# Grouped instance norm: 24 of 32 four-megabyte units joined to twelve of 8 MB, loaded as column halves, stored as whole rows

## The chip, the core and the metric

One core of a Trainium2 chip runs the kernel. The time is the device time of one execution, in microseconds; the three runs of the kernel before took 626.78, 626.83 and 626.91 us, median 626.83. The profile is of one further execution, recorded by the hardware profiler.

The engines named here: DVE (VectorE) and ACT (ScalarE) compute on data in SBUF, the on-chip memory of 128 partitions; PE (TensorE) multiplies matrices; POOL (GpSimd) does small set-up work; SP (SyncE) issues transfers. Transfers between HBM, the large memory, and SBUF are issued by SP, ACT or POOL, each on its own queue, and carried out by 16 DMA engines that serve all the queues.

## What is computed

```python
def reference(x, gamma):                       # x: 4 x 8 x 16 x 256 x 256, gamma: 8 x 16, float32
    mu = x.mean(axis=(3, 4), keepdims=True)
    var = ((x - mu) ** 2).mean(axis=(3, 4), keepdims=True)
    x_norm = (x - mu) / np.sqrt(var + 1e-5)
    out = x_norm * gamma[None, :, :, None, None]
    return out.astype(np.float32)
```

Each of the 4 x 8 x 16 = 512 channels has 65536 values (256 KB), is reduced to its mean and variance, and is written back normalised and scaled. Every value is read once and written once: 134.2 MB each way.

## The kernel before

**Tiling.** The input is seen as one flat array, cut into U = 32 units of 4 MB. A unit is 128 rows of F = 8192 values (32 KB); S = 8 rows are one channel, so a unit holds K = 16 channels, and it lies in one piece in HBM. Six SBUF tiles, `slots` (L45), are used in turn: unit u lives in slot u % 6.

**Order.** The order is written out by hand (`manual_schedule`): each engine takes its instructions as the program lists them, and waits where data or a buffer isn't there yet. At the start six loads are issued, those of units 1 and 3 on ACT's queue, the others on SP's (L56-57). Before them POOL issues two small transfers: `touch`, a write of 8 KB to the output (L54), and the load of gamma (L55). Then POOL builds `navg`, a 128 x 128 matrix that is -1/HW within each block of 8 rows (L63-72), and DVE and PE spread gamma over the partitions into `g_col` (L80-91).

**The loop over units** (L104-141), for each unit:

- L106: DVE sums each row. L107: ACT squares it and sums the squares (its full-size output, `junk`, is never read).
- L115: PE multiplies the two columns of sums by `navg`, which gives every row minus its channel's mean and minus its mean square, in PSUM.
- L116: DVE makes minus the variance; L120: ACT takes the root; L124 and L126: DVE inverts it and multiplies by gamma.
- L135: DVE adds minus the mean and multiplies by the scale, in place. In unit 0 alone, 3/8 of the columns go to ACT (L131-134).
- L139: ACT issues the store of the unit on its queue.
- L141: SP issues the load of unit u + 6 into the same slot, which must wait for that store to have landed.

So SP's queue carries the loads (but for two of the first), and ACT's queue all the stores. ACT issues a store only when DVE has finished L135, so the next unit's L107 stands behind it in ACT's program order. On DVE, the next unit's L106 stands behind L135.

Of the kernel before, what the change touches and what calls it, by code (L numbers as in the profile page):

```python
# [1 line left out]

# [4 lines left out]

F32 = mybir.dt.float32
U8 = mybir.dt.uint8
ALU = mybir.AluOpType  # L10
ACTF = mybir.ActivationFunctionType
AX = mybir.AxisListType


@with_exitstack
def kernel(
    ctx: ExitStack,
    tc: tile.TileContext,
    x: bass.AP,
    gamma: bass.AP,  # L20
    out: bass.AP,
):
    nc = tc.nc
    B, G, C, H, W = x.shape
    P = nc.NUM_PARTITIONS
    HW = H * W
    n_ch = B * G * C
    S = 8
    K = P // S
    F = HW // S  # L30
    U = n_ch // K
    NG = (G * C) // K
    AHEAD = 6
    assert HW % S == 0 and (G * C) % K == 0

    xv = x.rearrange("b g c h w -> (b g c h w)").rearrange("(u p f) -> u p f", p=P, f=F)
    ov = out.rearrange("b g c h w -> (b g c h w)").rearrange("(u p f) -> u p f", p=P, f=F)
    gv = gamma.rearrange("g c -> (g c)")

    data = ctx.enter_context(tc.tile_pool(name="data", bufs=1))  # L40
    singles = ctx.enter_context(tc.tile_pool(name="singles", bufs=1))
    psum = ctx.enter_context(tc.tile_pool(name="psum", bufs=4, space=bass.MemoryType.PSUM))
    ctx.enter_context(tc.manual_schedule())

    slots = [data.tile([P, F], F32, name=f"xt{i}") for i in range(AHEAD)]  # L45

    def load(u, queue):
        queue.dma_start(out=slots[u % AHEAD][:], in_=xv[u])  # L48


    g_row = singles.tile([1, G * C], F32, name="g_row")
    touch = singles.tile([16, 128], F32, name="touch")
    nc.vector.memset(touch[:], 0.0)  # L53
    nc.gpsimd.dma_start(out=ov[0][0::S, 0:128], in_=touch[:])  # L54
    nc.gpsimd.dma_start(out=g_row[:], in_=gv[None, :])  # L55
    for u in range(AHEAD):  # L56
        load(u, nc.scalar if u in (1, 3) else nc.sync)

    eps_t = singles.tile([P, 1], F32, name="eps_t")
    nc.gpsimd.memset(eps_t[:], 1e-5)  # L60
    one = singles.tile([1, 1], F32, name="one")
    nc.gpsimd.memset(one[:], 1.0)
    navg = singles.tile([P, K, S], F32, name="navg")  # L63
    nc.gpsimd.memset(navg[:], -1.0 / HW)  # L64
    nc.gpsimd.affine_select(  # L65
        out=navg[:], in_=navg[:], pattern=[[-S, K], [0, S]], compare_op=ALU.is_ge,
        fill=0.0, base=0, channel_multiplier=1,
    )
    nc.gpsimd.affine_select(  # L69
        out=navg[:], in_=navg[:], pattern=[[S, K], [0, S]], compare_op=ALU.is_ge,  # L70
        fill=0.0, base=S - 1, channel_multiplier=-1,
    )
    navg_w = navg[:].rearrange("p k s -> p (k s)")
    root_eps = singles.tile([P, 1], F32, name="root_eps")
    nc.scalar.activation(out=root_eps[:], in_=eps_t[:], func=ACTF.Sqrt)  # L75
    g_rep = singles.tile([1, NG, K, S], F32, name="g_rep")
    g_ps = psum.tile([P, NG], F32, name="g_ps", bufs=1)
    g_col = singles.tile([P, NG], F32, name="g_col")

    nc.vector.tensor_copy(  # L80
        out=g_rep[:],
        in_=g_row[:].rearrange("o (n k) -> o n k", n=NG).unsqueeze(3).to_broadcast([1, NG, K, S]),
    )
    for n in range(NG):
        nc.tensor.matmul(  # L85
            out=g_ps[:, n : n + 1],
            lhsT=g_rep[:, n].rearrange("o k s -> o (k s)"),
            rhs=one[:],
            start=True, stop=True,
        )  # L90
    nc.vector.tensor_copy(out=g_col[:], in_=g_ps[:])  # L91

    junk = singles.tile([P, F], U8, name="junk")

    st = singles.tile([P, U, 2], F32, name="st")
    nvar = singles.tile([P, U], F32, name="nvar")
    std = singles.tile([P, U], F32, name="std")
    rstd = singles.tile([P, U], F32, name="rstd")
    scale = singles.tile([P, U], F32, name="scale")

    shift = singles.tile([P, 1], F32, name="shift")

    squares = []
    for u in range(U):  # L104
        t = slots[u % AHEAD]
        nc.vector.reduce_sum(out=st[:, u, 0:1], in_=t[:], axis=AX.X)  # L106
        square = nc.scalar.activation(  # L107
            out=junk[:], in_=t[:], func=ACTF.Square, accum_out=st[:, u, 1:2],
        )
        if u:  # L110

            tc.declare_no_dep(square.ins, squares[-1].ins, reason="junk, ordered by the root between")
        squares.append(square)
        ps = psum.tile([P, 2], F32, name="ps")
        nc.tensor.matmul(out=ps[:], lhsT=navg_w, rhs=st[:, u], start=True, stop=True)  # L115
        nc.vector.tensor_scalar(  # L116
            out=nvar[:, u : u + 1], in0=ps[:, 0:1], scalar1=ps[:, 0:1],
            scalar2=ps[:, 1:2], op0=ALU.mult, op1=ALU.add,
        )
        nc.scalar.activation(  # L120
            out=std[:, u : u + 1], in_=nvar[:, u : u + 1], func=ACTF.Sqrt,
            bias=eps_t[:], scale=-1.0,
        )
        nc.vector.reciprocal(out=rstd[:, u : u + 1], in_=std[:, u : u + 1])  # L124
        g = u % NG
        nc.vector.tensor_mul(  # L126
            out=scale[:, u : u + 1], in0=rstd[:, u : u + 1], in1=g_col[:, g : g + 1],
        )
        cut = F * 5 // 8 if u == 0 else F
        if cut < F:  # L130
            nc.vector.tensor_mul(out=shift[:], in0=ps[:, 0:1], in1=scale[:, u : u + 1])  # L131
            nc.scalar.activation(  # L132
                out=t[:, cut:], in_=t[:, cut:], func=ACTF.Identity, bias=shift[:], scale=scale[:, u : u + 1],
            )
        nc.vector.tensor_scalar(  # L135
            out=t[:, :cut], in0=t[:, :cut], scalar1=ps[:, 0:1], scalar2=scale[:, u : u + 1],
            op0=ALU.add, op1=ALU.mult,
        )
        nc.scalar.dma_start(out=ov[u], in_=t[:])  # L139
        if u + AHEAD < U:  # L140
            load(u + AHEAD, nc.sync)  # L141


# [1 line left out]
_INS = ['x', 'gamma']  # L145
_OUTS = [((4, 8, 16, 256, 256), 'float32')]


# [23 lines left out]
```

## Time and profile before

| | |
|---|---|
| median of three runs | 626.83 us |
| the profiled execution, first to last instruction | 625.2 us |
| HBM read, written | 134.22 MB, 134.23 MB, 429 GB/s over the span |
| DVE busy | 441.8 us (71%) |
| ACT busy | 241.8 us (39%) |
| PE, POOL busy | 21.4 us, 2.4 us |
| L106, row sums (DVE) | 32 of 8.68 us |
| L107, squares (ACT) | 32 of 7.03 us |
| L135, normalise (DVE) | 31 of 4.55 us, one shorter |
| wait of L106 for loads | 102.2 us in 24 waits |
| wait of L107 for loads | 233.8 us in 24 waits |

The page of a profile shows the span in 40 equal slices (here 15.63 us each), with the mean busy share of the 16 DMA engines in tenths (9 is 90% or more) and what they moved in GB/s. It counts the packets of each DMA queue: q1 is SP's, q10 is ACT's. Its chain of waits goes back from the last instruction to what released it, step by step; lines of the chain read "start, duration, what". "To landing" is the time from the issue of a transfer to the completion signal, so it includes the time that the transfer stands in its queue. In a timeline a line reads "start, duration, engine, line, operation, output<-input", and the bracket is the idle time of that engine just before and what ended it.

### The profile page before, as it was taken

The page shows a single profiled execution, that of the slowest core. Times are in us where ns is not written, and L with a number is a line of the kernel's source. Part 1 is how long each engine was busy: PE and PEld are TensorE (multiplying, and loading weights), DVE is VectorE, ACT ScalarE, POOL GpSimd, SP SyncE. Part 2 cuts the span into 40 slices and gives each one's busy share as a digit, 9 for nine tenths or more (in the row PEclk, how much of TensorE's full clock was granted, in tenths as well). Part 3 has the DMA queues.
Part 4 walks back from the last instruction along what each step waited for, and adds up shares of the span by engine and source line. Part 5 has one row for each costly group of instructions (what it writes and reads, how often), then busy time and mean ns, then how long its engine had stood idle before and what let it go on. Part 6 is the DMA issues. An engine that isn't in the chain of part 4 may idle for free.

```text
span 625.2 us, 635 instructions
## 1 busy us (share of the span) xinstructions
PE 21.4 (3%) x80; PEld 19.5 (3%) x80; DVE 441.8 (71%) x164; ACT 241.8 (39%) x99; POOL 2.4 (0%) x11
## 2 busy tenths in 40 slices
PE   0200000000000000000000000000000000000000
PEld 0200000000000000000000000000000000000000
DVE  0589999998776687666786767867668676687730
ACT  0464444444443244432344423444224442244400
POOL 1000000000000000000000000000000000000000
DMA  8999999999999999999999999999999999999998
GB/s 370 436 407 432 436 436 436 436 436 430 423 436 434 434 428 434 434 436 436 436 436 428 426 436 436 432 430 434 434 436 436 436 436 421 432 436 434 434 430 367
DMA packets 9282, 268.46 MB, mean 429 GB/s; under 512 B 1072, under 2 KB 1088, under 8 KB 1088
## 3 DMA queue, kind: packets, MB, share of 16 engines
q10 hardware_dynamic: 4896, 142.61, 52.9%
q1 hardware_dynamic: 4320, 125.83, 46.8%
q0 software_dynamic: 64, 0.01, 0.0%
q14 instruction: 2, 0.02, 0.0%
HBM read 134.22 MB, written 134.23 MB: 429 GB/s over the span
## 4 chain that ended last, share of the span: by engine, by line
another core or an unknown queue 61%; DMA 17%; DVE 15%; SPq 1%; PE 1%; issue 0%; ACT 0%
DMA xt<-in_x_dram 10%; DVE st L106 10%; DMA out_dram<-xt 8%; DVE xt L135 5%; SPq L48 1%; PE ps L115 1%; ACT std L120 0%; DVE nvar L116 0%; DVE rstd L124 0%; DVE scale L126 0%; DVE shift L131 0%
## 5 line engine op out<-in xcount | busy, mean ns | idle before, releaser
L106 DVE TENSOR_REDUCE st<-xt 128x1 f32<-128x8192 f32 x32 | 277.9, 8684 | 102.2 <-DMA xt<-in_x_dram 102.2
L107 ACT ACTIVATE junk<-xt 128x8192 uint8<-128x8192 f32 x32 | 225.0, 7030 | 272.0 <-DMA xt<-in_x_dram 233.8
L135 DVE TENSOR_SCALAR xt<-xt,ps,scale 128x8192 f32<-128x8192 f32 (+1 forms) x32 | 144.0, 4500 | 1.1
L120 ACT ACTIVATE std<-nvar,eps_t 128x1 f32<-128x1 f32 x32 | 9.4, 295 | 79.4 <-DVE nvar L116 79.4
L115 PE MATMUL ps<-st,navg 128*128 128x2 f32 x64 | 17.8, 348 | 557.3 <-DVE st L106 557.3
L115 PEld LDWEIGHTS ps<-st,navg 128*128 128x128 f32 x64 | 16.0, 310 | 559.1 <-issue 546.2
L116 DVE TENSOR_SCALAR nvar<-ps 128x1 f32<-128x1 f32 x32 | 9.2, 286 | 23.8 <-PE ps L115 23.8
L124 DVE RECIPROCAL rstd<-std 128x1 f32<-128x1 f32 x32 | 5.2, 163 | 11.6 <-ACT std L120 11.6
L80 DVE COPY g_rep<-g_row 1x1024 f32<-1x1024 f32 x1 | 0.7, 681 | 14.4 <-DMA g_row<-in_gamma_dram 14.4
L107 ACT ACTIVATION_READ_ACCUMULATOR junk<-xt 128x1 f32 x32 | 6.0, 186 | 0.0
L126 DVE TENSOR_TENSOR scale<-rstd,g_col 128x1 f32<-128x1 f32 x32 | 5.1, 158 | 1.1
L85 PE MATMUL g_ps<-one,g_rep 1*128 1x1 f32 x16 | 3.5, 347 | 16.3 <-DVE g_rep L80 16.3
L85 PEld LDWEIGHTS g_ps<-one,g_rep 1*128 1x128 f32 x16 | 3.5, 326 | 16.3 <-issue 16.3
L132 ACT ACTIVATE xt<-xt,shift,scale 128x3072 f32<-128x3072 f32 x1 | 2.9, 2947 | 0.7 <-DVE shift L131 0.7
L91 DVE COPY g_col<-g_ps 128x8 f32<-128x8 f32 x1 | 0.2, 167 | 3.7 <-PE g_ps L85 3.7
L75 ACT ACT_TABLE_LOAD x1 | 1.3, 1283 | 1.7 <-PEq L156 1.7
L53 DVE MEMSET touch<- 16x128 f32 x1 | 0.2, 165 | 0.9 <-PEq L156 0.9
L54 POOL DMA_DIRECT2D out_dram<-touch x1 | 0.6, 617 | 0.8 <-DVE touch L53 0.8
L55 POOL DMA_DIRECT2D g_row<-in_gamma_dram x1 | 0.5, 487 | 0.0
L65 POOL TENSOR_SCALAR_AFFINE_SELECT navg<-navg 128x128 f32<-128x128 f32 x1 | 0.4, 400 | 0.1
L69 POOL TENSOR_SCALAR_AFFINE_SELECT navg<-navg 128x128 f32<-128x128 f32 x1 | 0.4, 399 | 0.1
L64 POOL MEMSET navg<- 128x128 f32 x1 | 0.2, 230 | 0.0
(8 smaller groups left out, 1.0 us busy)
## 6 DMA issues: line engine op xcount, KB each, us to landing
out_dram<-xt ACTq DMA_DIRECT2D x32, 4096.0 KB, 62.5
xt<-in_x_dram SPq DMA_DIRECT2D x30, 4096.0 KB, 38.5
xt<-in_x_dram ACTq DMA_DIRECT2D x2, 4096.0 KB, 31.7
out_dram<-touch POOLq DMA_DIRECT2D x1, 8.0 KB, 9.3
g_row<-in_gamma_dram POOLq DMA_DIRECT2D x1, 0.5 KB, 13.5
```

The source lines that it names most:

```text
L48: queue.dma_start(out=slots[u % AHEAD][:], in_=xv[u])
L75: nc.scalar.activation(out=root_eps[:], in_=eps_t[:], func=ACTF.Sqrt)
L85: nc.tensor.matmul(out=g_ps[:, n : n + 1], lhsT=g_rep[:, n].rearrange("o k s -> o (k s)"), rhs=one[:], start=True, stop=True,)
L106: nc.vector.reduce_sum(out=st[:, u, 0:1], in_=t[:], axis=AX.X)
L107: square = nc.scalar.activation(out=junk[:], in_=t[:], func=ACTF.Square, accum_out=st[:, u, 1:2],)
L115: nc.tensor.matmul(out=ps[:], lhsT=navg_w, rhs=st[:, u], start=True, stop=True)
L116: nc.vector.tensor_scalar(out=nvar[:, u : u + 1], in0=ps[:, 0:1], scalar1=ps[:, 0:1], scalar2=ps[:, 1:2], op0=ALU.mult, op1=ALU.add,)
L120: nc.scalar.activation(out=std[:, u : u + 1], in_=nvar[:, u : u + 1], func=ACTF.Sqrt, bias=eps_t[:], scale=-1.0,)
L124: nc.vector.reciprocal(out=rstd[:, u : u + 1], in_=std[:, u : u + 1])
L126: nc.vector.tensor_mul(out=scale[:, u : u + 1], in0=rstd[:, u : u + 1], in1=g_col[:, g : g + 1],)
L132: nc.scalar.activation(out=t[:, cut:], in_=t[:, cut:], func=ACTF.Identity, bias=shift[:], scale=scale[:, u : u + 1],)
L135: nc.vector.tensor_scalar(out=t[:, :cut], in0=t[:, :cut], scalar1=ps[:, 0:1], scalar2=scale[:, u : u + 1], op0=ALU.add, op1=ALU.mult,)
```

## The change

The unit list becomes uneven: four units of 4 MB ("singles"), twelve of 8 MB ("doubles"), and four singles again, 20 in all. F stays 8192. A double is 128 rows of 16384 values (64 KB), four rows to a channel, 32 channels.

- The six slots become three tiles of twice the width (`pairs`). `home(u)` gives a unit's tile and first column: a single takes one half of a tile, a double the whole.
- A double is loaded by two transfers of 4 MB, one for the left and one for the right half of the columns: each reads 32 KB out of every 64 KB of HBM. Each half is reduced and squared when it has come (inner loop over `halves`). PE adds both halves' sums up in one PSUM tile by two matmuls.
- The small steps (variance, root, reciprocal, scale) run once for a double. L135's successor normalises all 16384 columns in one instruction, and one transfer of 8 MB stores them in rows of 64 KB.
- The first loads are those of units 0 to 4: units 0 to 3 are singles and unit 4 is a double, which makes the same six transfers of 4 MB, on the same queues as before.
- A load is issued after the unit whose store frees the last of the halves that it needs. Loads of later doubles come two at a time on SP's queue; where singles follow doubles, the loads of two singles come together.
- The set-up builds `navg` and `g_col` twice, for 8 and for 4 rows to a channel.

```diff
@@ set-up, loads
-    S = 8
-    K = P // S
-    F = HW // S
-    U = n_ch // K
-    NG = (G * C) // K
-    AHEAD = 6
-    assert HW % S == 0 and (G * C) % K == 0
-    xv = x.rearrange("b g c h w -> (b g c h w)").rearrange("(u p f) -> u p f", p=P, f=F)
-    ov = out.rearrange("b g c h w -> (b g c h w)").rearrange("(u p f) -> u p f", p=P, f=F)
+    F = 8192
+    HALVES = 6
+    n_half = (B * G * C * HW) // (P * F)
+    ENDS = 4
+    assert n_half * P * F == B * G * C * HW and HW % (2 * F) == 0
+    sizes = [1] * ENDS + [2] * ((n_half - 2 * ENDS) // 2) + [1] * ENDS
+    starts = [sum(sizes[:i]) for i in range(len(sizes))]
+    assert sum(sizes) == n_half
+    xf = x.rearrange("b g c h w -> (b g c h w)")
+    of = out.rearrange("b g c h w -> (b g c h w)")
     gv = gamma.rearrange("g c -> (g c)")
+    def rows(flat, u):
+        n = sizes[u] * P * F
+        lo = starts[u] * P * F
+        return flat[lo : lo + n].rearrange("(p f) -> p f", p=P)
     data = ctx.enter_context(tc.tile_pool(name="data", bufs=1))
     singles = ctx.enter_context(tc.tile_pool(name="singles", bufs=1))
     psum = ctx.enter_context(tc.tile_pool(name="psum", bufs=4, space=bass.MemoryType.PSUM))
     ctx.enter_context(tc.manual_schedule())
-    slots = [data.tile([P, F], F32, name=f"xt{i}") for i in range(AHEAD)]
+    pairs = [data.tile([P, 2 * F], F32, name=f"xt{i}") for i in range(HALVES // 2)]
+    def home(u):
+        at = starts[u] % HALVES
+        return pairs[at // 2], (at % 2) * F
     def load(u, queue):
-        queue.dma_start(out=slots[u % AHEAD][:], in_=xv[u])
+        t, c = home(u)
+        src = rows(x_flat, u)
+        n = sizes[u] * F
+        step = F
+        for k in range(0, n, step):
+            queue.dma_start(out=t[:, c + k : c + k + step], in_=src[:, k : k + step])
+    x_flat, o_flat = xf, of
     g_row = singles.tile([1, G * C], F32, name="g_row")
     touch = singles.tile([16, 128], F32, name="touch")
     nc.vector.memset(touch[:], 0.0)
-    nc.gpsimd.dma_start(out=ov[0][0::S, 0:128], in_=touch[:])
+    nc.gpsimd.dma_start(out=rows(o_flat, 0)[0::8, 0:128], in_=touch[:])
     nc.gpsimd.dma_start(out=g_row[:], in_=gv[None, :])
-    for u in range(AHEAD):
+    first = [u for u in range(len(sizes)) if starts[u] + sizes[u] <= HALVES]
+    for u in first:
         load(u, nc.scalar if u in (1, 3) else nc.sync)
...
+    navg, g_col = {}, {}
+    for S in (8, 4):
+        K = P // S
+        w = singles.tile([P, K, S], F32, name=f"navg{S}")
+        nc.gpsimd.memset(w[:], -1.0 / HW)
+        nc.gpsimd.affine_select(
+            out=w[:], in_=w[:], pattern=[[-S, K], [0, S]], compare_op=ALU.is_ge,
+            fill=0.0, base=0, channel_multiplier=1,
+        )
+        nc.gpsimd.affine_select(
+            out=w[:], in_=w[:], pattern=[[S, K], [0, S]], compare_op=ALU.is_ge,
+            fill=0.0, base=S - 1, channel_multiplier=-1,
+        )
+        navg[S] = w[:].rearrange("p k s -> p (k s)")
     root_eps = singles.tile([P, 1], F32, name="root_eps")
     nc.scalar.activation(out=root_eps[:], in_=eps_t[:], func=ACTF.Sqrt)
-    g_rep = singles.tile([1, NG, K, S], F32, name="g_rep")
-    g_ps = psum.tile([P, NG], F32, name="g_ps", bufs=1)
-    g_col = singles.tile([P, NG], F32, name="g_col")
-    nc.vector.tensor_copy(
-        out=g_rep[:],
-        in_=g_row[:].rearrange("o (n k) -> o n k", n=NG).unsqueeze(3).to_broadcast([1, NG, K, S]),
-    )
-    for n in range(NG):
-        nc.tensor.matmul(
-            out=g_ps[:, n : n + 1],
-            lhsT=g_rep[:, n].rearrange("o k s -> o (k s)"),
-            rhs=one[:],
-            start=True, stop=True,
-        )
-    nc.vector.tensor_copy(out=g_col[:], in_=g_ps[:])
+    g_all = singles.tile([1, G * C * 8], F32, name="g_all")
+    for S in (8, 4):
+        K = P // S
+        n_g = (G * C) // K
+        g_rep = g_all[:, : G * C * S].rearrange("o (c s) -> o c s", s=S)
+        nc.vector.tensor_copy(
+            out=g_rep, in_=g_row[:].unsqueeze(2).to_broadcast([1, G * C, S]),
+        )
+        g_ps = psum.tile([P, n_g], F32, name=f"g_ps{S}", bufs=1)
+        g_col[S] = singles.tile([P, n_g], F32, name=f"g_col{S}")
+        for n in range(n_g):
+            nc.tensor.matmul(
+                out=g_ps[:, n : n + 1],
+                lhsT=g_all[:, n * P : (n + 1) * P],
+                rhs=one[:],
+                start=True, stop=True,
+            )
+        nc.vector.tensor_copy(out=g_col[S][:], in_=g_ps[:])
...
     for u in range(U):
-        t = slots[u % AHEAD]
-        nc.vector.reduce_sum(out=st[:, u, 0:1], in_=t[:], axis=AX.X)
-        square = nc.scalar.activation(
-            out=junk[:], in_=t[:], func=ACTF.Square, accum_out=st[:, u, 1:2],
-        )
-        if u:
-            tc.declare_no_dep(square.ins, squares[-1].ins, reason="junk, ordered by the root between")
-        squares.append(square)
+        t, c = home(u)
+        S = 8 // sizes[u]
+        halves = range(sizes[u])
+        for h in halves:
+            part = t[:, c + h * F : c + (h + 1) * F]
+            col = starts[u] + h
+            nc.vector.reduce_sum(out=st[:, col, 0:1], in_=part, axis=AX.X)
+            square = nc.scalar.activation(
+                out=junk[:], in_=part, func=ACTF.Square, accum_out=st[:, col, 1:2],
+            )
+            if squares and h == 0:
+                tc.declare_no_dep(square.ins, squares[-1].ins, reason="junk, ordered by the root between")
+            squares.append(square)
         ps = psum.tile([P, 2], F32, name="ps")
-        nc.tensor.matmul(out=ps[:], lhsT=navg_w, rhs=st[:, u], start=True, stop=True)
+        for h in halves:
+            nc.tensor.matmul(
+                out=ps[:], lhsT=navg[S], rhs=st[:, starts[u] + h],
+                start=h == 0, stop=h == sizes[u] - 1,
+            )
         nc.vector.tensor_scalar(
             out=nvar[:, u : u + 1], in0=ps[:, 0:1], scalar1=ps[:, 0:1],
             scalar2=ps[:, 1:2], op0=ALU.mult, op1=ALU.add,
...
-        g = u % NG
+        first_ch = starts[u] * (P // 8)
+        g = (first_ch % (G * C)) // (P // S)
         nc.vector.tensor_mul(
-            out=scale[:, u : u + 1], in0=rstd[:, u : u + 1], in1=g_col[:, g : g + 1],
-        )
-        cut = F * 5 // 8 if u == 0 else F
-        if cut < F:
+            out=scale[:, u : u + 1], in0=rstd[:, u : u + 1], in1=g_col[S][:, g : g + 1],
+        )
+        cut = F * 5 // 8 if u == 0 else sizes[u] * F
+        if cut < sizes[u] * F:
             nc.vector.tensor_mul(out=shift[:], in0=ps[:, 0:1], in1=scale[:, u : u + 1])
             nc.scalar.activation(
-                out=t[:, cut:], in_=t[:, cut:], func=ACTF.Identity, bias=shift[:], scale=scale[:, u : u + 1],
-            )
-        nc.vector.tensor_scalar(
-            out=t[:, :cut], in0=t[:, :cut], scalar1=ps[:, 0:1], scalar2=scale[:, u : u + 1],
-            op0=ALU.add, op1=ALU.mult,
-        )
-        nc.scalar.dma_start(out=ov[u], in_=t[:])
-        if u + AHEAD < U:
-            load(u + AHEAD, nc.sync)
+                out=t[:, c + cut : c + F], in_=t[:, c + cut : c + F], func=ACTF.Identity,
+                bias=shift[:], scale=scale[:, u : u + 1],
+            )
+        dst = rows(o_flat, u)
+        step = sizes[u] * F
+        for k in range(0, sizes[u] * F, step):
+            n = min(step, cut - k)
+            nc.vector.tensor_scalar(
+                out=t[:, c + k : c + k + n], in0=t[:, c + k : c + k + n], scalar1=ps[:, 0:1],
+                scalar2=scale[:, u : u + 1], op0=ALU.add, op1=ALU.mult,
+            )
+            nc.scalar.dma_start(out=dst[:, k : k + step], in_=t[:, c + k : c + k + step])
+        for v in range(len(first), U):
+            need = starts[v] + sizes[v] - HALVES
+            if starts[u] < need <= starts[u] + sizes[u]:
+                load(v, nc.sync)
```

`sizes` is 4 ones, 12 twos, 4 ones; `starts` is 0, 1, 2, 3, 4, 6, 8, ... 26, 28, 29, 30, 31. Between the parts of the loop that are shown, the lines for the variance, the root and the reciprocal are as before.

More of the change, by code (lines that the diff above doesn't have):

```diff
@@ L26 @@
     HW = H * W
-    n_ch = B * G * C
-    S = 8
-    K = P // S
-    F = HW // S
-    U = n_ch // K
-    NG = (G * C) // K
-    AHEAD = 6
-    assert HW % S == 0 and (G * C) % K == 0
-    xv = x.rearrange("b g c h w -> (b g c h w)").rearrange("(u p f) -> u p f", p=P, f=F)
-    ov = out.rearrange("b g c h w -> (b g c h w)").rearrange("(u p f) -> u p f", p=P, f=F)
+    F = 8192
[8 more added lines that the diff above has]
+    of = out.rearrange("b g c h w -> (b g c h w)")
     gv = gamma.rearrange("g c -> (g c)")
+    def rows(flat, u):
+        n = sizes[u] * P * F
+        lo = starts[u] * P * F
+        return flat[lo : lo + n].rearrange("(p f) -> p f", p=P)
     data = ctx.enter_context(tc.tile_pool(name="data", bufs=1))
@@ L62 @@
     nc.gpsimd.memset(one[:], 1.0)
[L63 to L67, printed above, removed]
-    )
-    nc.gpsimd.affine_select(
-        out=navg[:], in_=navg[:], pattern=[[S, K], [0, S]], compare_op=ALU.is_ge,
-        fill=0.0, base=S - 1, channel_multiplier=-1,
-    )
-    navg_w = navg[:].rearrange("p k s -> p (k s)")
+    navg, g_col = {}, {}
```

3 lines of the change are left out of this document (2 added, 1 removed).

## Prediction, made before the changed kernel was run

> **What bounds the kernel now.** I read the page's DMA slices first, then the queues, the chain of waits, the DVE timeline at the end, and SP's own waits.
>
> ```profile
> DMA  8999999999999999999999999999999999999998
> GB/s 370 436 407 432 436 436 436 436 436 430 423 436 434 434 428 434 434 436 436 436 436 428 426 436 436 432 430 434 434 436 436 436 436 421 432 436 434 434 430 367
> ...
> q10 hardware_dynamic: 4896, 142.61, 52.9%
> q1 hardware_dynamic: 4320, 125.83, 46.8%
> ...
> out_dram<-xt ACTq DMA_DIRECT2D x32, 4096.0 KB, 62.5
> xt<-in_x_dram SPq DMA_DIRECT2D x30, 4096.0 KB, 38.5
> ...
> out_dram<-touch POOLq DMA_DIRECT2D x1, 8.0 KB, 9.3
> g_row<-in_gamma_dram POOLq DMA_DIRECT2D x1, 0.5 KB, 13.5
> ```
>
> The sixteen DMA engines are full in every slice but the first and the last, while DVE is busy 71%. The bound is the DMA's total work. 142.61 MB in rows of 32 KB are 4352 packets of the store queue; the other 544 are the small ones that close each transfer.
>
> ```profile
> 198.57 0.02 SPq L48
> 198.60 0.03 issue
> 198.63 0.33 SPq L48
> 198.96 18.97 another core or an unknown queue
> 217.93 0.02 SPq L48
> ...
> 547.05 38.49 DMA xt<-in_x_dram
> 585.54 0.02 issue
> 585.57 8.70 DVE st L106
> ```
>
> The chain of waits repeats every 217.93 - 198.57 = 19.36 us: one 4 MB load plus one 4 MB store, 16 rows per DMA engine, so 1.21 us a row and 9.68 us a transfer when it has the engines alone. 32 periods are 619.5. The first load, queued beside another, lands at 22.75, 3.4 after 19.36 of rows; slice 3 at 407 against 436 lost 15.63 x 29/436 = 1.0, where the first store joins; 1.3 remain. Together 625.2, the span. The runs' median, 626.83, is 1.6 more, lying around the span; I add it unchanged.
>
> ```profile
> 585.56 7.03 ACT L107 ACTIVATE junk<-xt 128x8192 uint8<-128x8192 f32 x1 [9.30 <-DMA xt<-in_x_dram]
> ...
> 596.03 4.55 DVE L135 TENSOR_SCALAR xt<-xt,ps,scale 128x8192 f32<-128x8192 f32 x1
> 600.62 0.34 ACTq L139 DMA_DIRECT2D out_dram<-xt  x1
> ...
> SPq L48 <- DMA out_dram<-xt: 514.7, 26, 39.7
> ```
>
> The tail matters most. The last load lands at 585.54, its store is issued 15.1 later at 600.62, and the span ends at 625.2. In those 15.1 us the engines still run at full rate, because **about 39 us of stores are outstanding** at 585.5, of which 9.7 are the last unit's own. Stores take 62.5 us to land: over three are always queued. That depth hides the last unit's computation. SP's wait on stores shows that the queue's landing is also what frees a slot.
>
> **How the two queues share.** Loads (SP's queue) and stores (ACT's) advance in step now, both in 32 KB rows: the first two loads, one on each queue, land together only after 21.9 us. The touch lands at 1.36 + 9.3 = 10.7 and the 0.5 KB g_row at 1.98 + 13.5 = 15.5 behind it: 4.8 us = 4 x 1.21 for two tiny packets, each waiting for one 32 KB row of each other queue. So a turn is one packet, whatever its size. If a 64 KB row is one packet, a store takes two thirds of the engines while a load takes one third.
>
> **The change, part by part.**
> Row costs: a 64 KB row is not in the trace. From above it is two turns' worth, 2.42 us; from below 16 x 64 KB at the page's highest 436 GB/s, 2.405 us, which over 12 x 8 rows per engine is 1.4 us less. I take 2.42, the nearer row; ends -1.4 to 0.
>
> Issues: twelve fewer stores take 12 x 0.34 us from ACT's queue, hidden under DMA, worth nothing. The loads stay 32, but two go out back to back (0.33 each) when a double's store lands. Behind a waiting load on SP stand only later loads, and DVE waits for those.
>
> Computation: a single needs 15.1 from landing to store. A double needs 8.7 per half, 1.8 of small steps and 2 x 4.55 of L135: 28.3 on DVE against 2 x 15.1 = 30.1, and 19.6 from the second half's landing to the store. DVE at 71% hides that in mid-kernel. PE's matmul of the first half runs under the second reduce; 0.57 us remain, as now. Twelve sets of L116, L120, L124, L126 go, hidden by DMA.
>
> Start: POOL's second matrix costs 0.23 + 0.40 + 0.40 from 3.7 on, needed only near 80. The second gamma copy (half of 0.68), 8 passes (half of 3.54) and a 0.17 copy follow 20.06 and end near 22.7, just under the first landing at 22.75. Uncovered they delay DVE by some 0.5 us, which the four queued loads hide from DMA.
>
> Sharing: a store of 8 MB beside loads takes 8 x (2.42 + 1.21) = 29.0 us from issue when nothing is ahead of it, and one half-load passes meanwhile. Stores now leave quickly and wait no more; the buffered work moves to the load side. Carrying both queues forward by those turns (start 2.5, one loss of 1.0 at the first join, landing 1.1 after the last row, store issue as above) gives, in us; S is a single, D a double:
>
> ```
>       load lands (D: second)  store issued  store lands
> S3            43                   81           121
> D4            81                  109           150
> D5           120                  140           179
> D6           176                  197           226
> D7           198                  225           255
> D8           256                  276           306
> D9           276                  305           335
> D10          329                  349           378
> D11          358                  378           408
> D12          411                  431           461
> D13          430                  460           490
> D14          484                  504           533
> D15          513                  533           562
> S16          542                  557           582
> S17          568                  584           604
> S18          585                  601           614
> S19          605                  620           631
> ```
>
> The same bookkeeping with one-packet rows of 32 KB throughout puts the last load of the kernel before at 585.3 (585.54 in the trace) and its end at 624.9 (625.2).
>
> Sum: no gap before the tail, as one queue always has work. The last load lands near 604.7 instead of 585.5, with only S18's store left, which ends at 613.3. S19's first row starts at 620.3. **The DMA idles 7.0 us** that it doesn't now. Moving my two assumed lags (issue to first row 0.1 to 1.6, last row to landing 0.8 to 1.4) moves the gap only over 6.1 to 7.5. I take 6.6: 625.2 + 6.6 = 631.8 in the profile, 633.4 as a median. What would be late next is nothing: S19's store is last.
>
> **Rivals.**
> B, fair sharing: the 64 KB row is cut into two packets of 32 KB, or the engines share by bytes. Then the doubles do not do what they say, loads and stores stay in step, the store queue stays over two transfers deep, and the last load lands near 587, its 15.1 us covered. No gap: 626.7. For it: every packet of size in this trace is 32 KB, so nothing shows a 64 KB one. Against: the tiny packets' turns. It decides wherever the store queue does not lose 24 x 128 - 12 x 128 = 1536 of its row packets.
> C, rejoining: in the table the store queue runs dry and starts anew 6 to 9 times. If each start loses the 1.0 us of slice 3, the time is 633.4 + 6 to 9 = 639 to 642. Against: other queue changes, such as the loads' end near 585, show no dip of that size.
> D, cheaper transfers: fewer and longer rows at the 2.405 price, with fair sharing or a tail that stays covered: 626.8 - 1.4 = 625.4. It decides if stores are over a transfer and a half deep (15.1 us of rows) when the last load lands.
> E, dearer loads: half-loads read 32 KB at steps of 64 KB instead of running on. Bounds: nothing, or 24 x 9.68 x 29/436 = 15 us if all ran like slice 3, giving 633 to 649.
>
> On D: at 4.19 MB in 9.68 us the queue now moves 433 GB/s, within 0.06 us of the 436 rate per transfer. The Trainium skill (SBUF — State Buffer, The DMA setup-cost knee) gives each transfer a fixed 2 us and advises coalescing; twelve fewer would by that be an estimated 24 us, or 603. The trace disagrees: back to back, that cost is hidden, so I give it no chance beyond D's.
> On E: this trace has only contiguous tiles, so no row decides. The Trainium skill (DMA: Bandwidth & Descriptors, Latency and other measured facts) has large power-of-two row pitches slow copies, 207 GB/s at 512 KiB, restored to 214 by padding; 3% on 24 half-loads is an estimated 7 us more, 640. Its list starts well above 64 KB, so E stays small.
>
> **How the numbers follow.** Chances: forecast 0.60 (631.5 to 635), B 0.18, C 0.09, D 0.09, E 0.04. 0.2% of 626.83 is 1.25 us, about what a measurement here can tell from nothing. Slower: forecast, C, E and a little of B, 0.75. Same: most of B and a third of D, 0.17. Faster: 0.08. The range 626 to 638 holds the forecast and B and reaches toward C, leaving out most of C, D and E.
>
> **What would show it.** Right: the store queue loses 1536 row packets and its rows take about 2.4 us; store landing drops from 62.5 to near 30; the last load lands 600 or later; the last slices fall to about half rate. Wrong: the packet count unchanged, landings in step, the last load near 587; or losses spread along the slices (C, E), when the middle falls below 430.

## The result and the profile after

| | before | changed |
|---|---|---|
| median of four runs | 626.87 us (626.78 to 627.34) | 674.12 us (664.02 to 677.02) |
| ratio | | 1.0665, interval 1.0596 to 1.0735 |
| span of the profiled execution | 625.2 us | 671.7 us |

The ratio leaves out two of the changed kernel's runs that were disturbed (677.02 and 674.80 us), so it isn't that of the medians, and run 13 below leaves out its profiled execution in the same way (681.33 us, where its others are 651.85 to 652.95). The change makes the kernel slower by 6.7%; 633.4 had been forecast, with a range up to 638. The page of the changed kernel, the DMA lines of its slices, its queues and its transfers:

```profile
DMA  9999999999999999999999997999999999899865
GB/s 375 437 406 437 437 437 437 398 328 351 365 367 451 410 427 421 406 445 404 396 414 410 431 455 316 380 433 437 447 398 421 437 453 396 341 380 437 349 262 252
...
q10 hardware_dynamic: 3168, 142.61, 51.3%
q1 hardware_dynamic: 4320, 125.83, 44.8%
...
xt<-in_x_dram SPq DMA_DIRECT2D x30, 4096.0 KB, 52.0
out_dram<-xt ACTq DMA_DIRECT2D x8, 4096.0 KB, 32.3
...
out_dram<-xt ACTq DMA_DIRECT2D x12, 36.4
```

The store queue has 4896 - 3168 = 1728 packets fewer: the 1536 rows that were forecast and 12 x 16 closing ones. So a 64 KB row is one packet. From 119 to 192 us the trace has 256 store rows of 64 KB and 276 load rows of 32 KB, nearly one for one, so the stores get about two thirds of the bytes. Stores now land 32 to 36 us after issue, not 62.5: they run ahead of the loads, which take 52.0 in place of 38.5. A slice is 16.8 us here. Slices 8 to 12 (118 to 202 us) move 328 to 398 GB/s while the DMA engines are as busy as ever, and the last three are not full. The same in chosen stretches (each line reads start:end, length, busy time of PE, its weight loads, DVE, ACT and POOL, and ends with PE's clock, the busy share of the DMA engines and GB/s):

```profile
45.00:119.00 74.00, 3.17 (x12) 2.79 (x12) 67.88 (x21) 36.79 (x14) 0.00 (x0) 1.00 1.00 432
120.00:190.00 70.00, 1.11 (x4) 1.00 (x4) 26.80 (x6) 14.54 (x5) 0.00 (x0) 1.00 1.00 355
...
400.00:420.00 20.00, 0.56 (x2) 0.50 (x2) 18.82 (x6) 6.78 (x3) 0.00 (x0) 1.00 0.82 356
570.00:580.00 10.00, 0.00 (x0) 0.00 (x0) 10.00 (x2) 4.88 (x1) 0.00 (x0) 1.00 0.56 242
630.00:640.00 10.00, 0.56 (x2) 0.50 (x2) 8.82 (x5) 2.40 (x3) 0.00 (x0) 1.00 0.52 223
650.00:660.00 10.00, 0.56 (x2) 0.50 (x2) 8.27 (x5) 1.84 (x3) 0.00 (x0) 1.00 0.05 21
```

Two losses of different kind stand here. **Rows that take longer:** from 120 to 190 the engines are busy throughout (share 1.00) at 355 in place of 432 GB/s. **Engines without work:** in the last four stretches the share falls, and 3.6 + 4.4 + 4.8 + 9.5 = 22 us are idle.

The trace keeps every packet's duration. Added up and divided by the 16 engines, rows take 22 us more than in the kernel before (25.2 against 3.2 above 1.21 us for each 32 KB), and the engines are idle for 24.6 us more. Together that is the difference of the spans, 46.5. Of the 22 us, 13 fall between 119 and 192. There, a 64 KB store row takes 3.07 us on average (2.46 to 2.50 in the later parts of the run) and a 32 KB load row 1.38.

The end of the changed kernel:

```profile
598.90 8.69 DVE L135 TENSOR_REDUCE st<-xt 128x1 f32<-128x8192 f32 x1 [9.27 <-DMA xt<-in_x_dram]
...
624.98 8.69 DVE L135 TENSOR_REDUCE st<-xt 128x1 f32<-128x8192 f32 x1 [11.06 <-DMA xt<-in_x_dram]
...
640.04 0.34 ACTq L177 DMA_DIRECT2D out_dram<-xt  x1
644.42 8.69 DVE L135 TENSOR_REDUCE st<-xt 128x1 f32<-128x8192 f32 x1 [4.41 <-DMA xt<-in_x_dram]
654.89 4.55 DVE L173 TENSOR_SCALAR xt<-xt,ps,scale 128x8192 f32<-128x8192 f32 x1
659.48 0.34 ACTq L177 DMA_DIRECT2D out_dram<-xt  x1
```

The last load lands at 644.42 (585.54 before), and its store goes out 15.1 us later, as it did before. But by 644 only one store is left to do on fifteen of the engines, and 650 to 660 is almost empty.

**One engine is late.** The completions of a transfer, one for each of its 16 engines, stand in the trace one by one, and DVE starts on a load when the last of them is in (598.90, 624.98 and 644.42 above). For four transfers of the changed kernel, the times of the first, the eighth, the fifteenth and the last engine:

```
first   8th    15th   16th
388.8  389.0  403.6  439.3    a load, waited for until 439.33
553.8  553.9  558.5  598.9    a load, waited for until 598.90
610.1  610.2  610.3  625.0    a load, waited for until 624.98
629.4  629.5  629.7  644.4    the last load
```

In the kernel before, the last engine is at most 0.84 us behind the eighth (0.5 on average); here it is 9.5 us on average and up to 50. DVE, and with it every later store, waits for the last engine, while most of the others run dry. My reading of the records, which no run isolates: an engine that is late with a store still has store rows to do when the others have loads alone. Its load rows then pass at one per 3.6 us (2.42 + 1.21), in place of 1.2, so the lag grows.

### The profile page after: what moved, and what is told of

It reads as the page before. It is cut to its first block, busy times and chain, and to the rows that moved or that the text cites. A ratio compares the mean times of both kernels' runs of the same rounds, so it can differ in the third digit from the quotient of the medians.

```text
span 671.7 us, 585 instructions
## 1 busy us (share of the span) xinstructions
PE 23.3 (3%) x88; PEld 21.3 (3%) x88; DVE 430.8 (64%) x118; ACT 238.2 (35%) x87; POOL 3.6 (1%) x14
## 3 DMA queue, kind: packets, MB, share of 16 engines
q10 hardware_dynamic: 3168, 142.61, 51.3%
## 4 chain that ended last, share of the span: by engine, by line
DVE 44%; DMA 29%; another core or an unknown queue 22%; PE 1%; issue 1%; ACT 1%; SPq 0%
DVE st L135 28%; DMA xt<-in_x_dram 17%; DVE xt L173 14%; DMA out_dram<-xt 12%; PE ps L144 1%; ACT std L152 1%; DVE nvar L148 1%; SPq L64 0%; DVE rstd L156 0%; DVE scale L159 0%; DVE shift L164 0%
## 5 line engine op out<-in xcount | busy, mean ns | idle before, releaser
L135 DVE TENSOR_REDUCE st<-xt 128x1 f32<-128x8192 f32 x32 | 277.4, 8681 | 184.3 <-DMA xt<-in_x_dram 184.3
L173 DVE TENSOR_SCALAR xt<-xt,ps,scale 128x16384 f32<-128x16384 f32 (+2 forms) x20 | 140.6, 7030 | 0.7
L152 ACT ACTIVATE std<-nvar,eps_t 128x1 f32<-128x1 f32 x20 | 5.9, 295 | 54.6 <-DVE nvar L148 54.6
L148 DVE TENSOR_SCALAR nvar<-ps 128x1 f32<-128x1 f32 x20 | 5.7, 287 | 14.9 <-PE ps L144 14.9
L156 DVE RECIPROCAL rstd<-std 128x1 f32<-128x1 f32 x20 | 3.3, 164 | 7.2 <-ACT std L152 7.2
L109 PE MATMUL g_ps<-one,g_all 1*128 1x1 f32 x24 | 5.4, 348 | 16.7 <-DVE g_all L103 16.7
L109 PEld LDWEIGHTS g_ps<-one,g_all 1*128 1x128 f32 x24 | 5.3, 324 | 16.8 <-issue 16.1
L159 DVE TENSOR_TENSOR scale<-rstd,g_col 128x1 f32<-128x1 f32 x20 | 3.2, 159 | 0.7
```

What stands on the lines that cost most here:

```text
L109: nc.tensor.matmul(out=g_ps[:, n : n + 1], lhsT=g_all[:, n * P : (n + 1) * P], rhs=one[:], start=True, stop=True,)
L135: nc.vector.reduce_sum(out=st[:, col, 0:1], in_=part, axis=AX.X)
L148: nc.vector.tensor_scalar(out=nvar[:, u : u + 1], in0=ps[:, 0:1], scalar1=ps[:, 0:1], scalar2=ps[:, 1:2], op0=ALU.mult, op1=ALU.add,)
L152: nc.scalar.activation(out=std[:, u : u + 1], in_=nvar[:, u : u + 1], func=ACTF.Sqrt, bias=eps_t[:], scale=-1.0,)
L159: nc.vector.tensor_mul(out=scale[:, u : u + 1], in0=rstd[:, u : u + 1], in1=g_col[S][:, g : g + 1],)
L173: nc.vector.tensor_scalar(out=t[:, c + k : c + k + n], in0=t[:, c + k : c + k + n], scalar1=ps[:, 0:1], scalar2=scale[:, u : u + 1], op0=A ...
```

## The experiments

Line numbers and names are those of the changed kernel where nothing else is said; each time is a median beside runs of the kernel before on the same chip (626.8 to 627.3).

**1. Stores in column halves.** All rows are 32 KB; halves are normalised and stored one by one.

```diff
         dst = rows(o_flat, u)
-        step = sizes[u] * F
+        step = F
```

> Doubles stored as two column halves, 32 KB rows at steps of 64 KB, so every row in both queues is 32 KB. Turn theory (a 64 KB row takes one turn, so stores run ahead of loads): shares are equal again, the stores stay queued, no gap; 626 to 629 us, the last load lands before 595. Row-price theory (64 KB rows cost 3 us beside loads): also cured, 626 to 629, rows 1.21 us. Pitch theory (half-rows at steps of 64 KB are slow): not cured, 650 us or more, with rows above 1.3 us.

Measured: 627.74 us, ratio 1.0006 (0.9997 to 1.0016). The whole loss is gone. The slices of its page:

```profile
GB/s 369 435 421 427 427 433 435 435 435 435 435 434 421 434 435 435 435 435 429 429 433 435 435 433 435 435 435 423 431 435 435 435 433 431 429 433 435 435 432 339
```

Its timeline at the end, the last load's reduce and store:

```profile
585.43 8.69 DVE L135 TENSOR_REDUCE st<-xt 128x1 f32<-128x8192 f32 x1 [4.35 <-DMA xt<-in_x_dram]
...
600.48 0.34 ACTq L177 DMA_DIRECT2D out_dram<-xt  x1
```

The last load lands at 585.43, 0.1 us earlier than in the kernel before, and no slice sags. Both queues now step 64 KB in HBM between rows, and rows still take 1.21 us, so the pitch (the step from one row to the next) costs nothing here. The pitch theory falls.

**2. Loads of doubles in whole rows,** 64 KB in both queues.

```diff
         n = sizes[u] * F
-        step = F
+        step = n
```

> Doubles loaded by one transfer of 8 MB in rows of 64 KB, stored as before in rows of 64 KB. Turn theory: both queues have 64 KB rows, shares are equal, the store queue stays deep, 627 to 634 us (the load of a whole double comes 8 MB at a time). Row-price theory: 64 KB rows are dear beside other traffic, now in both queues; 650 us or more. Pitch theory: no half-rows are left, 627 to 634.

Measured: 638.20 us, ratio 1.0168 (1.0142 to 1.0193): the figures of all three theories missed. 64 KB rows take their 2.42 us (means 2.45 and 2.43), so they aren't dear by themselves. But the last load is waited for until 610.52, the tail is uncovered, and some 9 us more are idle than in the kernel before. Here too the engines are apart: the eighth had the last load at 597.6, the fifteenth at 604.6, the last at 610.5. How much of the loss is that spread and how much the coarser units of 8 MB isn't shown. Its slices:

```profile
GB/s 377 442 399 432 440 405 415 446 448 407 456 428 424 452 411 444 436 424 444 415 448 415 444 440 415 452 419 444 440 415 448 424 421 434 424 417 389 428 316 265
```

and the last reduce and store in its timeline:

```profile
610.52 8.69 DVE L135 TENSOR_REDUCE st<-xt 128x1 f32<-128x8192 f32 x1 [4.35 <-DMA xt<-in_x_dram]
...
625.57 0.34 ACTq L177 DMA_DIRECT2D out_dram<-xt  x1
```

**3. Whole rows for loads, halves for stores:** both edits above together, so the longer rows are the loads'.

```diff
-        step = F
+        step = n
...
-        step = sizes[u] * F
+        step = F
```

> Loads of doubles in 64 KB rows, stores in halves of 32 KB: the sizes of the two queues exchanged. Turn theory: loads now take two turns' worth to the stores' one, the stores stay queued deeper than in the kernel before, the tail is covered, 626 to 632 us. Row-price theory: 64 KB rows cost about 3 us beside the other queue, 650 us or more. Pitch theory: the half-row stores are slow, 640 us or more.

Measured: 629.73 us, ratio 1.0040 (1.0025 to 1.0055). The turn theory's time holds: the same two row sizes, exchanged, cost under 3 us, and idle time is within 1.1 us of the kernel before. The deeper store queue that it expected isn't there: stores land after 43.4 us, as in run 1, where the kernel before has 62.5.

**4. Contiguous loads,** store rows as in the change.

```diff
-            queue.dma_start(out=t[:, c + k : c + k + step], in_=src[:, k : k + step])
+            lo = (starts[u] * F + k) * P
+            queue.dma_start(out=t[:, c + k : c + k + step], in_=x_flat[lo : lo + P * F].rearrange("(p f) -> p f", p=P))
```

> The changed kernel, but each 4 MB load of a double reads one contiguous 4 MB block (rows of 32 KB one behind the other) in place of half of every 64 KB row; the rows then hold other values, so the output is not the reference's. Stores keep 64 KB rows. Turn theory and row-price theory: no change from the changed kernel, 660 to 680 us. Pitch theory: cured of the slow rows, 627 to 640.

Measured: 672.37 us, ratio 1.0708 (1.0673 to 1.0743), with the same sag to 350 GB/s in the same slices. The pitch theory falls a second time.

**5. Normalised whole, then stored by two transfers** with 32 KB rows.

```diff
-            nc.scalar.dma_start(out=dst[:, k : k + step], in_=t[:, c + k : c + k + step])
+            for m in range(k, k + step, F):
+                nc.scalar.dma_start(out=dst[:, m : m + F], in_=t[:, c + m : c + m + F])
```

> The changed kernel in everything (normalised whole, stored only then) but that the 8 MB store is issued as two transfers one behind the other, the column halves, in rows of 32 KB. If it is the size of the store's row that costs the time: cured, 627 to 630 us. If it is that 8 MB are stored at once, after the whole double is normalised: not cured, 650 us or more.

Measured: 627.75 us, ratio 1.0008 (0.9998 to 1.0017). That a double is stored only when it is normalised whole costs nothing. With run 1 this leaves the row size of the store.

**6. A second load queue** beside 64 KB store rows.

```diff
         for k in range(0, n, step):
+            q = nc.gpsimd if k and u > 4 else queue
-            queue.dma_start(out=t[:, c + k : c + k + step], in_=src[:, k : k + step])
+            q.dma_start(out=t[:, c + k : c + k + step], in_=src[:, k : k + step])
```

> The changed kernel with its 64 KB store rows, but from unit 5 on the right half of each double is loaded on POOL's queue, so loads have two queues of 32 KB rows against one of 64 KB. Turn theory: loads get two turns for each store's one, shares are equal again while both load queues hold work, stores stay queued; 628 to 640 us. Row-price theory: a 64 KB store row is slow beside any 32 KB load row; 645 us or more, rows near 3 us.

Measured: 638.50 us, ratio 1.0173 (1.0141 to 1.0205), within the turn theory's figures. The stores' 64 KB rows stay as they were, and the slow stretch is gone:

```profile
120.00:190.00 70.00, 1.67 (x6) 1.50 (x6) 40.25 (x11) 18.26 (x8) 7.66 (x2) 1.00 1.00 433
200.00:560.00 360.00, 10.60 (x38) 9.52 (x38) 250.21 (x59) 134.17 (x48) 3.70 (x7) 1.00 1.00 432
```

The store rows take 2.43 us on average, beside 32 KB load rows on two queues. So a 64 KB store row beside 32 KB load rows isn't slow in itself. From 210 to 300 us, some 32 store rows of 64 KB and 64 load rows pass in 10 us, equal shares of the bytes. The run changes the number of queues together with the shares, and doesn't separate the two. What is left is mostly idle time, some 9 us more than in the kernel before, at the end as in run 2.

**7 and 8. The ratio without any 64 KB row, first try.** The kernel before; loads in two column halves of 16 KB rows (7), stores too (8).

```diff
-        queue.dma_start(out=slots[u % AHEAD][:], in_=xv[u])
+        for k in range(0, F, F // 2):
+            queue.dma_start(out=slots[u % AHEAD][:, k : k + F // 2], in_=xv[u][:, k : k + F // 2])
```

> The kernel before, 4 MB units, each load split into two column halves in rows of 16 KB; stores keep rows of 32 KB. No 64 KB row is left, but the ratio of the rows is 2 to 1 as in the changed kernel. Turn theory: the stores run ahead, the last load lands near 608 in place of 585, about 10 us idle at the end: 633 to 645 us. Row-price theory (64 KB rows): no change, 626 to 629 us.

> The kernel before, loads and stores both split into two column halves in rows of 16 KB: the ratio is 1 to 1 and rows are half as long. Both theories: 626 to 630 us; it prices the shorter rows alone.

Measured: 650.98 us (ratio 1.0379, 1.0352 to 1.0406) and 641.40 us (1.0226, 1.0211 to 1.0241). Both are above every figure given for them. The control, run 8, missed by 11 us, so the pair is inconclusive: with twice as many transfers ACT waits for earlier stores before it can go on, which it never did in the kernel before. From ACT's waits of run 8 (us in total, times, longest):

```profile
ACT junk L108 <- DMA out_dram<-xt: 220.5, 20, 11.4
```

**9 and 10. The same, without more transfers.** Each 4 MB transfer moves two 16 KB pieces a partition, loads alone (9) or both (10).

```diff
+    xk = x.rearrange("b g c h w -> (b g c h w)").rearrange("(u k p f) -> u p k f", k=2, p=P, f=F // 2)
...
-        queue.dma_start(out=slots[u % AHEAD][:], in_=xv[u])
+        queue.dma_start(out=slots[u % AHEAD][:].rearrange("p (k f) -> p k f", k=2), in_=xk[u])
```

> The kernel before, 32 loads of 4 MB as before, but each in two pieces of 16 KB a partition (the unit's first and second 2 MB), so load rows are 16 KB against store rows of 32 KB in as many transfers as before; the partitions then hold other values, so the output is not the reference's. Turn theory: stores take two thirds, the last load lands near 608, 10 us idle at the end, 635 us; with rows slowed as in the first doubles' stretch up to 655. If only rows of 64 KB do harm: 626 to 629.

> The same with the stores in two pieces of 16 KB a partition too: every row is 16 KB, the ratio 1 to 1, transfers as many as before (groups of rows are then averaged with others' channels, so the output is not the reference's). Turn theory: 626 to 630, stores land after about 62 us again. It prices 16 KB rows without the added transfers of the earlier pair of runs.

Measured: 649.35 us (1.0356, 1.0326 to 1.0386) and 629.81 us (1.0055, 1.0038 to 1.0071). The two differ in the stores' rows alone: the ratio of 2 to 1 costs 19.5 us in the 4 MB kernel, without a 64 KB row or a double. The transfers on the page of run 9:

```profile
out_dram<-xt ACTq DMA_DIRECT2D x32, 4096.0 KB, 19.7
xt<-in_x_dram SPq DMA_DIRECT2D x30, 4096.0 KB, 78.8
```

and its stretch from 620 to 640:

```profile
620.00:640.00 20.00, 0.56 (x2) 0.50 (x2) 13.85 (x5) 7.42 (x3) 0.00 (x0) 1.00 0.36 152
```

Stores land after 19.7 us where the control has 62.8; the last load is waited for until 622.41, where 608 was expected, and 13 of the 20 us from 620 on are idle. Here too the engines are apart: the eighth had that load at 610.1. The rows are slowed by only 6 us against the control.

**11 to 14. Few doubles.** Only the list of sizes is changed: the first double alone; one double behind 16 singles; the first two; two with ten singles between.

```diff
-    sizes = [1] * ENDS + [2] * ((n_half - 2 * ENDS) // 2) + [1] * ENDS
+    sizes = [1] * ENDS + [2] * 1 + [1] * (n_half - ENDS - 2)
...
+    sizes = [1] * 16 + [2] + [1] * (n_half - 18)
...
+    sizes = [1] * ENDS + [2] * 2 + [1] * (n_half - ENDS - 4)
...
+    sizes = [1] * 4 + [2] + [1] * 10 + [2] + [1] * (n_half - 18)
```

> The changed kernel with only its first double. By the turns alone the store queue keeps about two transfers, the last load lands near 594, its computation is covered, no idle at the end: 626 to 628. With slow rows while its one 64 KB store runs (29 us at 350 in place of 433 GB/s): 5 to 7 us more, 631 to 635.

> One double only, as the run with the first double alone, but in the middle: after 16 singles, with 14 behind it. If the slowed rows belong to a 64 KB store that runs beside loads while both queues hold work and all engines go in step: the same cost again, 631 to 636 us, rows near 2.9 us, last load near 594 plus 6. If they belong to the early part of the run or to those addresses: 626 to 628.

> The changed kernel with only its first two doubles; all other units are singles with 32 KB rows in both queues. If the loss is made anew by each double, a sixth of the 47 us: 634 us. If the depth of the store queue, once lost, is not made up while the shares are equal: the last load lands near 604, about 6 us idle at the end, and with the slow rows of the first stretch (13 us) 640 to 648 us.

> Two doubles as in the run with the first two, but ten singles apart. If the stores' lead, once won, stays through the singles and the second double adds to it: the last load lands near 604 plus the slowed rows, idle at the end, 640 to 655 us, as for two doubles side by side (652.8). If the ten singles restore the queue: twice one double's cost, 638 to 642.

| | median | ratio | last load waited for until |
|---|---|---|---|
| first double alone | 633.81 us | 1.0116 (1.0101 to 1.0132) | 601.90 |
| one behind 16 singles | 633.40 us | 1.0105 (1.0090 to 1.0120) | 601.60 |
| first two | 652.77 us | 1.0407 (1.0390 to 1.0424) | profile not used |
| two, ten singles apart | 644.09 us | 1.0281 (1.0252 to 1.0310) | 614.74 |

The first two doubles side by side took more than either figure given for them (634, or 640 to 648). The stretch of the one store and what follows it, where the first double stands alone:

```profile
120.00:155.00 35.00, 0.56 (x2) 0.50 (x2) 17.41 (x6) 7.42 (x3) 0.00 (x0) 1.00 0.99 368
160.00:560.00 400.00, 11.71 (x42) 10.52 (x42) 286.87 (x105) 152.28 (x63) 0.00 (x0) 1.00 1.00 433
```

The same where one double stands behind 16 singles:

```profile
355.00:385.00 30.00, 0.56 (x2) 0.50 (x2) 11.96 (x5) 5.53 (x3) 0.00 (x0) 1.00 1.01 378
390.00:600.00 210.00, 6.14 (x22) 5.52 (x22) 150.36 (x55) 80.07 (x33) 0.00 (x0) 1.00 1.00 433
```

Two doubles, ten singles apart: the stretches of both, then the tail:

```profile
120.00:155.00 35.00, 0.56 (x2) 0.50 (x2) 17.43 (x6) 7.42 (x3) 0.00 (x0) 1.00 1.00 368
350.00:385.00 35.00, 1.12 (x4) 1.00 (x4) 25.86 (x11) 14.84 (x6) 0.00 (x0) 1.00 1.00 427
600.00:620.00 20.00, 0.56 (x2) 0.50 (x2) 13.49 (x6) 7.06 (x4) 0.00 (x0) 1.00 0.96 408
620.00:630.00 10.00, 0.56 (x2) 0.50 (x2) 8.59 (x5) 2.15 (x3) 0.00 (x0) 1.00 0.27 116
```

One double costs 7 us at either place, with the DMA at 368 or 378 GB/s during its store and full before and after. Slowed rows make 5.3 us of it in the first run and 4.2 in the second; the rest is idle time, 1.3 and 2.1 us more than in the kernel before. So the loss doesn't belong to the early part of the run or to those addresses. After it the last load is at 601.9: 16.4 us later than in the kernel before, of which 5.3 are the slowed rows. The rest, 11.1, is a lead of the stores of about one transfer (9.68 us), which 26 singles with equal shares don't take back. The second double adds to the lead: the last load is waited for until 614.74, its store goes out at 629.79, and 620 to 630 is three quarters idle. The expectation of a lead that stays through singles held.

What stays open is why the rows stretch. They do where a 64 KB store follows straight on a queued store, beside 32 KB loads of one queue, with the 16 engines less than 4 us apart. They don't in the pair's second stretch (427 GB/s), where the engines lie 4 to 5 us apart (346.7 to 351.2 for the transfer that ends just before) and the store queue had less ahead of it. In the changed kernel the rows of the first two doubles' stores take 3.05 and 3.08 us on average, those of the other ten 2.42 to 2.53. The third double's take 2.43: its store is issued at 211.10, when the store queue has run dry, and the engines (200.4 to 202.9) are no further apart than at the end of the slow stretch (189.4 to 191.9). So the spread of the engines alone doesn't decide it; whether the depth of the store queue does wasn't tried.

## Why the prediction failed, point by point

**Held.** The bound is the DMA, and a packet is a turn whatever its size: 1536 row packets fewer, store landing from 62.5 to 36, loads later, and an uncovered tail. Runs 1, 3, 6 and 9 show it from four sides. The forecast gap before the last store is there, 9.5 us between 650 and 660 where 7.0 was forecast, but it is a fifth of the 46.5 us. Run 2, with equal shares and 11 us lost, shows that the shares don't account for everything. The costs set at nothing were nothing: with equal shares (runs 1 and 5) the doubles, the second gamma copy and the doubled loads on SP together come to under 1 us. DVE's normalising of a double took 8.82 us, where 9.10 was used.

**The step that failed first: "I take 2.42, the nearer row".** The price of a 64 KB row was bounded by -1.4 to 0 us from rows that ran beside equals. Its mean is 2.57, the load rows beside it rose to 1.25, and together they lost 22 us that the sum lacks. Runs 11 and 12 price it for one double: 4 to 5 us of slowed rows, 7 us in all. In run 6, beside two load queues, the 2.42 holds.

**The step that failed next: the sixteen engines as one.** "No gap before the tail, as one queue always has work" holds for each engine only while all get their share at the same time. Here one fell up to 50 us behind. In place of one gap of 7.0 us the trace has four, together 22, two of them before 600 us. The last load, put at 604.7, was waited for until 644.4, though fifteen engines had it at 629.7.

**Rivals.** B (two packets to a row) is excluded by the count. C, one loss at each rejoin of the store queue, isn't settled: 9 of the 22 us of slower rows lie outside the first stretch, 4 of them between 290 and 400, and they were not tried alone. But the first and largest loss came while the store queue had never run dry, and the third double's store, which starts on an empty queue, has rows of 2.43 us. D: the shorter list of transfers gained nothing in any run. E, dearer half-rows, fell with runs 1 and 4. The Trainium skill's rule on row pitch (DMA: Bandwidth & Descriptors, Latency and other measured facts) was rightly kept small: at 64 KB no run shows it (627.74 us in run 1).

Of the signs that the prediction named, most of those for right came (the packets, the landings, the last load after 600, the last slices), and one for wrong came too: middle slices below 430, such as 316 and 341. That sign stood for C and E, and neither of them is one of these two losses. The range ended at 638 because each unknown price was bounded alone, and two things had no bound: a 64 KB row dearer than two of 32 KB, and engines that fall out of step.

## What to carry to other kernels

Where loads and stores share saturated DMA engines, a queue's share follows its row length, so compare the rows of both queues before joining one of them: the stores' rows twice the loads' cost 20 to 47 us here, the reverse under 3. In this kernel a deep store queue is what hides the last unit's computation, and a lead that stores had won once was not taken back by equal shares afterwards. A transfer lands with its slowest engine: look at the sixteen completions when a wait is longer than the bytes explain.

## What the runs showed of the hardware that was not expected

Busy DMA engines that move less: 355 GB/s over 70 us, share 1.00, where store rows of 64 KB and load rows of 32 KB alternate and take 3.07 and 1.38 us in place of 2.42 and 1.21. One engine of sixteen 50 us behind on a load that the others had finished, in a program that gives all the same rows. And rows of 16 KB in both queues cost 3.0 us in all (629.81 against 626.78): 512 more rows per engine, 6 ns each. From 32 to 64 KB about as little is gained: half of the changed kernel's 64 KB rows take 2.418 us or less, and two of 32 KB take 2 x 1.213 = 2.426.
